# Pinning the adaLN dot-product passes behind the weights' subtractions on VectorE

## The chip, the cores and the metric

One core of a Trainium2 chip runs the whole kernel in one launch. The metric is device time in microseconds; lower is better. All inputs are in HBM in fp32 and the output is written back there.

## The reference, cut to what matters

Two layers work on 256 latent and 256 context tokens of width 2048. Each layer modulates its normalised input with vectors that are a matrix product of a conditioning vector and a large weight (adaLN), goes through a wide projection, a mixer and an output projection:

```python
for layer in range(DEPTH):                       # 2
    shift, scale, gate = split(silu(c) @ ada_w[layer] + ada_b[layer], 3)      # ada_w: 2048 x 6144
    h = rms_norm(x, pre_g[layer]) * (1.0 + scale) + shift                     # the same for ctx with c_ctx
    if layer % 2 == 0:
        y = pool_conv_mixer(h, ev_w_in, ..., ev_w_out)   # 2048 -> 6144, mixer, 2048 -> 2048
    else:
        y, yc = hgrn2_mixer(h, hc, od_w_in, ..., od_w_out)
    x = x + gate * rms_norm(y, post_g[layer])
```

`silu(c) @ ada_w` has only two rows (latent and context), so it is a matrix-vector product for each of two vectors; every weight is used twice.

## The kernel before, in words

Activations stand as 16 tiles of 128 features by 512 tokens. Every large product is done in three TensorE matmuls of 128x512 for each 128x128 block (`mm3`, lines 172 to 174): the fp32 weight tile `raw` is split into a rounded part `whi` (a cast on ScalarE, line 131) and a rest `wlo` (**the weights' subtraction** on VectorE, line 132), and the products whi·x_hi, whi·x_lo and wlo·x_hi are added in PSUM. The third matmul, L174, is the only one that needs `wlo`.

- **Weights' stream.** `order` lists every weight load of the program; `weights()` hands out the next split tile and `ahead()` starts the load, the cast and the subtraction of the one after it. `raw`, `whi` and `wlo` have 3 buffers each. `proj_tile` computes one output tile of 128 features in two **halves**; a half takes one weight tile of 128x1024 and 24 matmuls.
- **Stages.** First the group product of 7 feature tiles (`main0`, weights `evg`), then feature tiles 7 to 47 of the even layer's input projection (weights `ev`, 82 halves), with the pooling mixer (`finish_a`, lines 500 to 561) and the convolution mixer (`finish_b`, lines 571 to 582) in between; then its output projection (weights `evo`, 16 tiles, 32 halves; `yin` is its input, lines 627 to 635 gather sums of each tile); then the odd layer.
- **adaLN on VectorE.** Part of the adaLN products is no TensorE work: `ada_dve` (line 257) loads transposed weights `adat` 128x1024 at a time into the two buffers `raw2` (512 KB each; `loads` asks for the next one before it hands out the last) and multiplies and sums each with `srow`, once for each of the two vectors: `tensor_tensor_reduce`, line 270, called **a pass** here. The profile shows a pass as a custom instruction that writes `ajunk` and a short accumulator read behind it. One load with its two passes is called **a part**. There are 104 parts, 208 passes. `step(n)` runs the next n parts at places in the source: six in the last `main0` calls, two in each half from feature tile 7 on until the first 16 are done, then, with `hook0`, one in the second half of feature tiles 12, 13 and 17, one in each half from feature tile 18 on, and one in each half of the output projection until they are used up. `add_shift` (lines 420 and 421) adds a shift to h around the end of feature tile 11 and needs the first 16 parts.
- **Order.** A scheduler at build time puts each engine's instructions in a fixed order by its own estimate of when their inputs are there. Nothing ties a pass to its place in the source: it may stand before or after subtractions and mixer work of other places. On the chip each engine and the queue of loads on SyncE run strictly in the order built.

Of the kernel before, what the change touches and what calls it, by code (L numbers as in the profile page):

```python
# [12 lines left out]
ALU = mybir.AluOpType  # L13
# [34 lines left out]
def block_kernel(ctx: ExitStack, tc: tile.TileContext, par, xt, invcnt, poolw, ada, adat, crow, evg, evb, ev, evo,  # L48
                 odg, odz, odi, odo, rows, out):
    nc = tc.nc  # L50
    V, S, GP, T = nc.vector, nc.scalar, nc.gpsimd, nc.tensor
# [9 lines left out]
    def mm_ps(nm="mmps"):  # L61
        return ps.tile([P, 512], F32, name=nm, tag="mm", bufs=5)

    def aux_ps(shape, nm):
        return ps.tile(shape, F32, name=nm, tag="aux", bufs=3)
# [49 lines left out]
    def loads(srcs):  # L115

        t = None
        for src in srcs:
            nx = load(src, "raw2", 2)
            if t is not None:  # L120
                yield t
            t = nx
        yield t
# [91 lines left out]
    def ada_end(l, t, k0, tr):  # L215

        nk, nv = tr.shape[1:]
        ks = slice(k0, k0 + nk)
        m = mod[:, l, t, ks, 0:nv]
        V.tensor_tensor(m, tr, ada_b[:, l, t, ks].unsqueeze(2).broadcast_to([P, nk, nv]), op=ALU.add)  # L220
        if t == 0:
            return
        if t == 1:
            V.tensor_scalar(m, m, 1.0, None, op0=ALU.add)
        g = (pre_g if t == 1 else post_g)[:, l, ks]
        V.tensor_tensor(m, m, g.unsqueeze(2).broadcast_to([P, nk, nv]), op=ALU.mult)
# [26 lines left out]
    srow = a0.tile([P, 2, D], F32, name="srow")  # L253
# [6 lines left out]
    def ada_dve(units):  # L260

        parts = [(l, t, 4 * u + i, half) for l, t, u in units for i in range(4) for half in range(2)]
        srcs = [adat[ADAT[l, t], n, :, half * 1024:half * 1024 + 1024] for l, t, n, half in parts]
        for (l, t, n, half), raw in zip(parts, loads(srcs)):
            i = n % 4
            if not i and not half:
                sums = a0.tile([P, 2, 4, 2], F32, name="asum", bufs=2)
            for v in range(2):
                junk = a0.tile([P, 1024], BF16, name="ajunk")
                V.tensor_tensor_reduce(junk, raw, srow[:, v, half * 1024:half * 1024 + 1024], 1.0,  # L270
                                       sums[:, 0, i, v:v + 1] if half else 0.0, op0=ALU.mult, op1=ALU.add,
                                       accum_out=sums[:, half, i, v:v + 1])
            if half and i == 3:
                ada_end(l, t, n - 3, sums[:, 1])
            yield
# [69 lines left out]
    def ada_raw(l, t, u, s):  # L345
        raw = big_tile([P, 4, 1024], F32, "adaraw")
        for g in range(0, 4, 2):
            nc.sync.dma_start(raw[:, g:g + 2, :],
                              ada[l, t, u, 4 * s + g:4 * s + g + 2].rearrange("g p n -> p g n"))
        return raw  # L350
# [25 lines left out]
    for u in range(1, 4):  # L376
        acc = aux_ps([P, P], "adaps")
        for s in range(2):
# [5 lines left out]
            raw = ada_raw(0, 1, u, s)  # L384
# [5 lines left out]
        make_h0(range(4 * u, 4 * u + 4))  # L390

    job = ada_dve([(0, 0, u) for u in range(2, 4)])

    for u in range(2):
        acc = aux_ps([P, P], "adaps")
        for s in range(2):
            raw = ada_raw(0, 0, u, s)
# [62 lines left out]
    def bias_job():  # L460
# [7 lines left out]
        yield  # L468

    job = ada_dve([(0, 2, u) for u in range(4)] + [(1, t, u) for u in range(4) for t in (1, 0) if t == 0 or u < 3])  # L470

    LP = 8
# [181 lines left out]
    sums = [mm_ps("stps") for _ in range(3)]  # L654
# [414 lines left out]
    half = [[mm_ps() for _ in range(2)] for _ in range(2)]  # L1069
# [16 lines left out]
    half = [[mm_ps(), aux_ps([P, 512], "mmx")], [aux_ps([P, 512], "mmx") for _ in range(2)]]  # L1086
# [112 lines left out]
```

## Time and profile before

| | us |
|---|---|
| median of 3 runs | 1710.59 (1707.89 to 1714.49) |
| profiled execution, device time | 1711.67 |
| its span, first to last instruction | 1710.0 |
| TensorE busy | 1648.6 (96%) |
| TensorE weight loads busy | 1356.4 (79%) |
| VectorE busy | 1193.2 (70%) |
| ScalarE busy | 595.8 (35%) |
| bytes moved | 295.28 MB, mean 173 GB/s |

The profiled execution lies 1.1 us above the median and 1.67 us of it are outside the span. Busy time is the union of instructions on an engine; matmul records overlap (a 128x512 matmul is shown as 0.39 us though the next starts 0.23 us later), so a busy TensorE is not one at its peak. "Idle before" is put down to what ended it.

### The profile page before, as it was taken

The page shows a single profiled execution, that of the slowest core. Times are in us where ns is not written, and L with a number is a line of the kernel's source. Part 1 is how long each engine was busy: PE and PEld are TensorE (multiplying, and loading weights), DVE is VectorE, ACT ScalarE, POOL GpSimd, SP SyncE. Part 2 cuts the span into 40 slices and gives each one's busy share as a digit, 9 for nine tenths or more (in the row PEclk, how much of TensorE's full clock was granted, in tenths as well). Part 3 has the DMA queues.
Part 4 walks back from the last instruction along what each step waited for, and adds up shares of the span by engine and source line. Part 5 has one row for each costly group of instructions (what it writes and reads, how often), then busy time and mean ns, then how long its engine had stood idle before and what let it go on. Part 6 is the DMA issues. An engine that isn't in the chain of part 4 may idle for free.

```text
span 1710.0 us, 23085 instructions
## 1 busy us (share of the span) xinstructions
PE 1648.6 (96%) x8878; PEld 1356.4 (79%) x8878; DVE 1193.2 (70%) x2079; ACT 595.8 (35%) x944; POOL 79.3 (5%) x154
## 2 busy tenths in 40 slices
PE   7999999998999999999799999999999999999997
PEld 4777778876777788887688888888888888888886
DVE  3459988998888844444996873778648774566755
ACT  4323533322122223332353432343323332434543
POOL 0000000000000000001300000000000100000000
PEclk9999999999999999999899999999999999999999
DMA  9986466666666663333266542545425333333453
GB/s 355 351 333 223 153 217 196 209 220 211 221 208 213 214 255 108 99 99 121 67 169 180 166 156 86 179 148 183 143 87 186 116 103 107 114 120 112 167 183 130
DMA packets 98046, 295.28 MB, mean 173 GB/s; under 512 B 26000, under 2 KB 26128, under 8 KB 96272
## 3 DMA queue, kind: packets, MB, share of 16 engines
q1 hardware_dynamic: 97936, 293.82, 52.0%
q8 instruction: 69, 1.13, 0.3%
q14 instruction: 41, 0.34, 0.1%
HBM read 289.58 MB, written 4.19 MB: 172 GB/s over the span
## 4 chain that ended last, share of the span: by engine, by line
PE 66%; DVE 15%; DMA 13%; issue 5%; POOL 0%; ACT 0%; SPq 0%; DVEq 0%; POOLq 0%; ACTq 0%
PE mmps L172 12%; PE mmps L173 12%; PE mmps L174 12%; DMA raw<-adat_dram 9%; PE mmps L191 5%; DVE ajunk L270 5%; PE mmps L952 3%; PE mmps L954 3%; PE mmps L953 3%; DVE wlo L132 3%; PE mmps L192 3%; DMA raw<-ada_dram 1%; DMA adaraw<-ada_dram 1%; PE adaps L212 1%; PE mmps L1061 1%
## 5 line engine op out<-in xcount | busy, mean ns | idle before, releaser
L132 DVE TENSOR_TENSOR wlo<-raw,whi 128x1024 fp32r<-128x1024 f32 (+3 forms) x328 | 388.6, 1187 | 284.7 <-ACT whi L131 277.6
L131 ACT CAST whi<-raw 128x1024 fp32r<-128x1024 f32 (+3 forms) x328 | 334.3, 1024 | 720.6 <-PE mmps L173 455.7
L174 PE MATMUL mmps<-h,wlo 128*128 128x512 f32 x1216 | 478.2, 394 | 22.7 <-DVE wlo L132 22.6
L172 PE MATMUL mmps<-h,whi 128*128 128x512 f32 x1216 | 479.4, 395 | 7.2 <-ACT h L710 6.6
L173 PE MATMUL mmps<-h,whi 128*128 128x512 f32 x1216 | 478.6, 394 | 3.8 <-DVE h L711 3.6
L174 PEld LDWEIGHTS mmps<-h,wlo 128*128 128x128 f32 x1216 | 230.1, 189 | 80.0 <-DVE wlo L132 32.3
L172 PEld LDWEIGHTS mmps<-h,whi 128*128 128x128 f32 x1216 | 230.2, 189 | 58.3 <-ACT h L710 7.2
L173 PEld LDWEIGHTS mmps<-h,whi 128*128 128x128 f32 x1216 | 230.5, 190 | 52.6 <-DVE h L711 4.9
L191 PE MATMUL mmps<-h,whi 128*128 128x512 f32 x496 | 177.9, 401 | 0.0
L270 DVE CUSTOM_DVE_ANT_0 ajunk<-raw,srow,asum 128x1024 bf16<-128x1024 f32 x104 | 133.4, 1283 | 30.4 <-DMA raw<-adat_dram 29.1
L192 PE MATMUL mmps<-h,wlo 128*128 128x256 f32 x496 | 139.4, 281 | 1.3 <-DVE wlo L132 1.3
L270 DVE CUSTOM_DVE_ANT_0 ajunk<-raw,srow 128x1024 bf16<-128x1024 f32 x104 | 127.1, 1222 | 16.9 <-DMA raw<-adat_dram 16.0
L191 PEld LDWEIGHTS mmps<-h,whi 128*128 128x128 f32 x496 | 93.1, 188 | 23.0 <-issue 0.5
L952 PE MATMUL mmps<-whi,h 128*128 128x512 f32 x256 | 100.1, 391 | 0.0
L954 PE MATMUL mmps<-wlo,h 128*128 128x512 f32 x256 | 99.8, 390 | 0.0
L953 PE MATMUL mmps<-whi,h 128*128 128x512 f32 x256 | 99.8, 390 | 0.0
L172 PE MATMUL mmps<-yin,whi 128*128 128x512 f32 x256 | 99.6, 389 | 0.0
L173 PE MATMUL mmps<-yin,whi 128*128 128x512 f32 x256 | 99.6, 389 | 0.0
L174 PE MATMUL mmps<-yin,wlo 128*128 128x512 f32 x256 | 99.6, 389 | 0.0
L192 PEld LDWEIGHTS mmps<-h,wlo 128*128 128x128 f32 x496 | 93.6, 189 | 2.6 <-DVE wlo L132 2.0
L954 PEld LDWEIGHTS mmps<-wlo,h 128*128 128x128 f32 x256 | 48.1, 188 | 10.2
L174 PEld LDWEIGHTS mmps<-yin,wlo 128*128 128x128 f32 x256 | 48.1, 188 | 10.0
(271 smaller groups left out, 1966.9 us busy)
## 6 DMA issues: line engine op xcount, KB each, us to landing
raw<-odz_dram SPq DMA_DIRECT2D x118, 512.0 KB, 3.3
raw<-adat_dram SPq DMA_DIRECT2D x104, 512.0 KB, 4.6
raw<-ev_dram SPq DMA_DIRECT2D x82, 512.0 KB, 4.5
adaraw<-ada_dram SPq DMA_DIRECT2D x24, 1024.0 KB, 8.9
raw<-ada_dram SPq DMA_DIRECT2D x36, 512.0 KB, 4.3
raw<-evo_dram SPq DMA_DIRECT2D x32, 512.0 KB, 3.4
raw<-odi_dram SPq DMA_DIRECT2D x32, 512.0 KB, 3.4
raw<-odo_dram SPq DMA_DIRECT2D x32, 512.0 KB, 3.3
```

What stands on the lines that cost most here:

```text
L131: S.copy(hi[:, 0:n], raw[:, 0:n])
L132: V.tensor_tensor(lo[:, 0:n], raw[:, 0:n], hi[:, 0:n].bitcast(F32), op=ALU.subtract)
L172: T.matmul(o, whi, xhi, start=first, stop=False)
L173: T.matmul(o, whi, xlo, start=False, stop=False)
L174: T.matmul(o, wlo, xhi, start=False, stop=last)
L191: T.matmul(o, whi, xhl, start=first, stop=False)
L192: T.matmul(o[:, 0:SEQ], wlo, xhl[:, 0, :], start=False, stop=last)
L212: T.matmul(acc[32 * j:32 * j + 32, :], vec[:, k, :], rv[:, i, j, :], start=k == 0, stop=k == KT - 1, tile_position=(0, 32 * j))
L270: V.tensor_tensor_reduce(junk, raw, srow[:, v, half * 1024:half * 1024 + 1024], 1.0, sums[:, 0, i, v:v + 1] if half else 0.0, op0=ALU.mult ...
L952: T.matmul(o, xh[:, c], hi[:, w], start=k == 0, stop=False)
L953: T.matmul(o, xl[:, c], hi[:, w], start=False, stop=False)
L954: T.matmul(o, xh[:, c], lo[:, w], start=False, stop=k == KT - 1)
```

## The change

Each pass is wrapped in a call that adds an edge of order, without a wait, from the instruction traced just before it on VectorE. A pass can then not be placed ahead of anything that the source has before it on VectorE; what the source has behind it can still be placed ahead of it.

```diff
             for v in range(2):
                 junk = a0.tile([P, 1024], BF16, name="ajunk")
-                V.tensor_tensor_reduce(junk, raw, srow[:, v, half * 1024:half * 1024 + 1024], 1.0,
-                                       sums[:, 0, i, v:v + 1] if half else 0.0, op0=ALU.mult, op1=ALU.add,
-                                       accum_out=sums[:, half, i, v:v + 1])
+                tc.keep_in_program_order(V.tensor_tensor_reduce(
+                    junk, raw, srow[:, v, half * 1024:half * 1024 + 1024], 1.0, sums[:, 0, i, v:v + 1] if half else 0.0,
+                    op0=ALU.mult, op1=ALU.add, accum_out=sums[:, half, i, v:v + 1]))
```

The instructions are the same ones; their order moves. VectorE in the middle of the even layer's input projection, before (L132 is a weights' subtraction, a row that writes ajunk is a pass, the row behind it its accumulator read, other lines are mixer work):

```order
L132 TENSOR_TENSOR wlo<-raw,whi 128x1024
L270 ISA ajunk,asum<-raw_3411,srow 128x1024
L270 ISA asum 128x1
L270 ISA ajunk,asum<-raw_3411,srow 128x1024
L270 ISA asum 128x1
L270 ISA ajunk,asum<-raw_3447,srow,asum 128x1024
L270 ISA asum 128x1
L270 ISA ajunk,asum<-raw_3447,srow,asum 128x1024
L270 ISA asum 128x1
L132 TENSOR_TENSOR wlo<-raw,whi 128x1024
```

The same passes with the change:

```order
L132 TENSOR_TENSOR wlo<-raw,whi 128x1024
L270 ISA ajunk,asum<-raw_3411,srow 128x1024
L270 ISA asum 128x1
L270 ISA ajunk,asum<-raw_3411,srow 128x1024
L270 ISA asum 128x1
L132 TENSOR_TENSOR wlo<-raw,whi 128x1024
L270 ISA ajunk,asum<-raw_3447,srow,asum 128x1024
L270 ISA asum 128x1
L270 ISA ajunk,asum<-raw_3447,srow,asum 128x1024
L270 ISA asum 128x1
L571 TENSOR_TENSOR ubuf_1756<-mmps,bc 128x256 x2
L132 TENSOR_TENSOR wlo<-raw,whi 128x1024
```

Where two to four passes stood between two subtractions, two stand now, all the way down the stage. Between the subtraction of feature tile 20's second half and that of tile 47's second half there were 154 passes, and there are 110. VectorE in the output projection, before (L630 and L635 are the sums of a finished tile):

```order
L132 TENSOR_TENSOR wlo<-raw,whi 128x1024 x2
L630 TENSOR_TENSOR sqy<-yb,xb 128x512
L635 TENSOR_TENSOR acc_4896<-acc_4896,sqy 128x512
L635 TENSOR_TENSOR acc_4897<-acc_4897,sqy 128x512
L635 TENSOR_TENSOR acc_4898<-acc_4898,sqy 128x512
L132 TENSOR_TENSOR wlo<-raw,whi 128x1024 x2
```

With the change:

```order
L132 TENSOR_TENSOR wlo<-raw,whi 128x1024
L630 TENSOR_TENSOR sqy<-yb,xb 128x512
L635 TENSOR_TENSOR acc_4896<-acc_4896,sqy 128x512
L635 TENSOR_TENSOR acc_4897<-acc_4897,sqy 128x512
L635 TENSOR_TENSOR acc_4898<-acc_4898,sqy 128x512
L270 ISA ajunk,asum<-raw_5154,srow,asum 128x1024
L270 ISA asum 128x1
L270 ISA ajunk,asum<-raw_5154,srow,asum 128x1024
L270 ISA asum 128x1
L132 TENSOR_TENSOR wlo<-raw,whi 128x1024
L270 ISA ajunk,asum<-raw_5190,srow 128x1024
L270 ISA asum 128x1
```

Before, no pass stood here; now 54 do, two behind each subtraction of output tiles 0 to 13. On SyncE's queue the `adat` loads move along: 154 and 110 passes mean 77 and 55 loads beside the `ev` loads, and 27 now alternate with the `evo` loads, on both sides of the four 1 MB loads of `xb` (line 614). VectorE around `add_shift` (L421), before:

```order
L435 COPY sh_pad<-mod 128x16x2
L523 COPY pm<-pm 128x256
L270 ISA ajunk,asum<-raw_1796,srow 128x1024
L270 ISA asum 128x1
L132 TENSOR_TENSOR wlo<-raw,whi 128x1024
L421 SCALAR_TENSOR_TENSOR h_195<-xr,mod,h_193 128x256 x16
L421 SCALAR_TENSOR_TENSOR h_196<-xr,mod,h_194 128x256 x9
L270 ISA ajunk,asum<-raw_1798,srow,asum 128x1024
L270 ISA asum 128x1
L421 SCALAR_TENSOR_TENSOR h_196<-xr,mod,h_194 128x256 x7
L132 TENSOR_TENSOR wlo<-raw,whi 128x1024 x3
```

With the change:

```order
L132 TENSOR_TENSOR wlo<-raw,whi 128x1024
L220 TENSOR_TENSOR mod<-asum,pt 128x8
L421 SCALAR_TENSOR_TENSOR h_195<-xr,mod,h_193 128x256 x16
L421 SCALAR_TENSOR_TENSOR h_196<-xr,mod,h_194 128x256 x9
L435 COPY sh_pad<-mod 128x16x2
L501 COPY psum_w<-psum_w 128x2
L500 TENSOR_TENSOR psum_w<-psum_w 128x556
L421 SCALAR_TENSOR_TENSOR h_196<-xr,mod,h_194 128x256 x7
L501 COPY psum_w<-psum_w 128x4
L521 TENSOR_TENSOR pm<-psum_w 128x128
L132 TENSOR_TENSOR wlo<-raw,whi 128x1024 x2
```

The passes of later parts (raw_1796, raw_1798) left this place, and some pooling work took theirs.

## Rows read from the trace of the kernel before

**Rows 1.** The page: busy time, and shares of the chain that ended last.

```profile
PE 1648.6 (96%) x8878; PEld 1356.4 (79%) x8878; DVE 1193.2 (70%) x2079; ACT 595.8 (35%) x944; POOL 79.3 (5%) x154
...
PE mmps L172 12%; PE mmps L173 12%; PE mmps L174 12%; DMA raw<-adat_dram 9%; PE mmps L191 5%; DVE ajunk L270 5%; PE mmps L952 3%; PE mmps L954 3%; PE mmps L953 3%; DVE wlo L132 3%; PE mmps L192 3%; DMA raw<-ada_dram 1%; DMA adaraw<-ada_dram 1%; PE adaps L212 1%; PE mmps L1061 1%
```

**Rows 2.** Busy time by stretch: columns as in the first row.

```profile
core 0: us, PE busy (x) PEld busy (x) DVE busy (x) ACT busy (x) POOL busy (x), PEclk, DMA share, GB/s
...
245.00:370.00 125.00, 125.00 (x552) 103.30 (x551) 114.13 (x191) 38.35 (x55) 0.00 (x0) 1.00 0.64 204
370.00:592.00 222.00, 203.99 (x863) 162.35 (x863) 193.26 (x301) 46.92 (x54) 0.00 (x0) 0.98 0.67 214
592.00:800.00 208.00, 207.69 (x917) 171.71 (x916) 95.38 (x125) 69.44 (x104) 0.00 (x0) 1.00 0.39 132
```

**Rows 3.** Costliest groups in 370 to 592 us.

```profile
L174 PE MATMUL mmps<-h,wlo 128*128 128x512 f32 x287 | 115.1, 401 | 18.0 <-DVE wlo L132 17.9
...
L270 DVE CUSTOM_DVE_ANT_0 ajunk<-raw,srow,asum 128x1024 bf16<-128x1024 f32 x55 | 70.6, 1284 | 19.2 <-DMA raw<-adat_dram 18.4
L270 DVE CUSTOM_DVE_ANT_0 ajunk<-raw,srow 128x1024 bf16<-128x1024 f32 x54 | 66.0, 1222 | 9.5 <-DMA raw<-adat_dram 8.9
...
L132 DVE TENSOR_TENSOR wlo<-raw,whi 128x1024 fp32r<-128x1024 f32 x36 | 43.9, 1220 | 0.0
```

**Rows 4.** Waits of VectorE in 370 to 592 us: total, times, longest.

```profile
DVE ajunk L270 <- DMA raw<-adat_dram: 27.3, 33, 1.8
```

**Rows 5.** Timeline, 382 to 392 us: start, duration, engine, instruction, idle before it.

```profile
382.44 1.05 ACT L131 CAST whi<-raw 128x1024 fp32r<-128x1024 f32 x1 [4.34 <-PE mmps L173]
...
384.69 1.22 DVE L270 CUSTOM_DVE_ANT_0 ajunk<-raw,srow 128x1024 bf16<-128x1024 f32 x1
...
387.21 1.28 DVE L270 CUSTOM_DVE_ANT_0 ajunk<-raw,srow,asum 128x1024 bf16<-128x1024 f32 x1 [1.29 <-DMA raw<-adat_dram]
...
389.75 1.22 DVE L132 TENSOR_TENSOR wlo<-raw,whi 128x1024 fp32r<-128x1024 f32 x1
...
391.02 0.50 PE L174 MATMUL mmps<-h,wlo 128*128 128x512 f32 x1 [2.48 <-DVE wlo L132]
```

**Rows 6.** TensorE by windows: us, PE busy (x), clock, DMA share, GB/s.

```profile
440.00:450.00 10.00, 9.66 (x36) 0.83 0.71 224
450.00:460.00 10.00, 10.00 (x46) 1.00 0.73 237
```

**Rows 7.** Weights and adat loads in 370 to 592 us: time from issue to landing.

```profile
DMA to landing us min/median/max: 3.2/4.6/6.5
```

**Rows 8.** VectorE in 660 to 704 us, costliest groups: four output tiles.

```profile
L132 DVE TENSOR_TENSOR wlo<-raw,whi 128x1024 fp32r<-128x1024 f32 x9 | 11.0, 1225 | 28.3 <-ACT whi L131 28.3
L635 DVE TENSOR_TENSOR acc<-acc,sqy 128x512 f32<-128x512 f32 x12 | 7.6, 684 | 0.0
L630 DVE TENSOR_TENSOR sqy<-yb,xb 128x512 f32<-128x512 f32 x4 | 2.7, 684 | 0.0
```

**Rows 9.** Busy time by stretch in the output projection, columns as in rows 2.

```profile
620.00:640.00 20.00, 20.00 (x90) 16.58 (x89) 7.36 (x9) 7.08 (x10) 0.00 (x0) 1.00 0.84 326
640.00:700.00 60.00, 60.00 (x267) 49.69 (x266) 26.62 (x35) 20.31 (x31) 0.00 (x0) 1.00 0.33 106
```

**Rows 10.** Timeline of TensorE and VectorE before and around add_shift.

```profile
130.70 0.50 PE L174 MATMUL mmps<-h,wlo 128*128 128x512 f32 x1 [1.08 <-DVE wlo L132]
...
179.61 9.99 DVE L421 SCALAR_TENSOR_TENSOR h<-xr,mod,h 128x256 fp32r<-128x256 f32 x25
...
193.49 3.50 DVE L132 TENSOR_TENSOR wlo<-raw,whi 128x1024 fp32r<-128x1024 f32 x3
...
194.77 0.53 PE L174 MATMUL mmps<-h,wlo 128*128 128x512 f32 x1 [3.35 <-DVE wlo L132]
```

**Rows 11.** Waits of VectorE in 120 to 245 us: total, times, longest.

```profile
DVE wlo L132 <- ACT whi L131: 4.2, 3, 2.4
```

## The prediction

> **What bounds the kernel now.** I read the page first. TensorE is busy for 1648.6 of 1710.0 us, so idle time alone offers 61 us; but the chain that ended last spends 9% of the span on `adat` loads, 5% on passes and 3% on subtractions [rows 1]. That names a place where TensorE waits for VectorE, which waits for a load of the adaLN job.
>
> Busy time by stretch shows where [rows 2]. From 592 to 800 us TensorE does 917 matmuls in 208 us, from 245 to 370 us 552 in 125 us: 0.2268 and 0.2264 us each, the rate of a fed engine. From 370 to 592 us it does 863 in 222 us. At 0.2266 us they need 195.6 us, so **26.4 us are lost in this stretch**. The 863 are 36 halves of 24 matmuls: 6.17 us for a half where 5.44 would do.
>
> The costliest groups of that stretch say who is late [rows 3]. The only TensorE group that waits is L174, the matmul that needs `wlo`: 18.0 us, all but 0.1 put down to the subtraction. VectorE does 36 subtractions and 55 + 54 = 109 passes there, three for each half where the source has two. It is busy for 193.26 us [rows 2] and waits 27.3 us for `adat` loads [rows 4]: 220.6 of 222 us. So VectorE, with those waits, is the bound here and TensorE follows.
>
> One stall in the timeline [rows 5] shows how. The cast of a weight tile ends at 383.49 us, so its subtraction could start. Two passes stand ahead of it, then 1.29 us of waiting for the next part's load, then two more passes; the subtraction starts at 389.75 us, and TensorE stands idle 2.48 us until 391.02.
>
> The matmul-busy row shows 18.0 us of idle, the count of matmuls 26.4. The rest lies in matmul records that overlap across a stall and in the clock: granted 0.98 in the stretch [rows 2], a loss of at most 222 x 0.02 = 4.4 us; in 440 to 450 us, behind one stall of 2 us, it is 0.83 and 36 matmuls pass in 9.66 busy us, 46 in the 10 us after at 1.00 [rows 6]. If only the visible idle came back, the gain would be 18 us and the time 1693. I take the count. The Trainium skill, in Perfetto Trace Analysis, Identifying the Most-Contended Engine, says that matmul busy time is a bad measure and that weight-load busy time should be read. By that rule, 162.35 us of weight loads against 171.71 in 208 us of a fed stretch [rows 2] would need 196.7 us, a loss of 25.3; the trace agrees with the rule and not with the busy row.
>
> **The change, part by part.**
>
> *Projection of the even layer, 370 to 592 us.* No instruction is added or removed. Between subtractions stand two passes instead of three on average, so these 36 halves lose 109 - 72 = 37 passes. A pass lasts 1.22 or 1.28 us [rows 3]; at 1.25, 46 us leave, and VectorE has 193.3 - 46 = 147 us of work, 4.1 us in each half of 5.44. The subtraction comes first in its half, and 1.3 us are over. The waits for loads shrink as well. A part now takes 222 / 54.5 = 4.07 us, so a `raw2` buffer comes round every 8.15 us, of which its two passes take 2.5 and a load 4.6 [rows 7], with about 1 us of waiting and issue between. At a part for each half it comes round every 10.88 us, 2.7 us later than now, against a mean wait of 27.3 / 54.5 = 0.5 us [rows 4] and a longest of 1.8. I expect all 26.4 us back.
>
> *Moved into the output projection: 27 parts.* They land on 592 to 800 us, where VectorE is busy for 95 of 208 us [rows 2]. An output tile takes TensorE 10.88 us. VectorE there has two subtractions, 2.45 us, and sums of (7.6 + 2.7) / 4 = 2.6 us [rows 8]; four passes of 1.25 make it 10.0. That is tight but fits, and the cover is deeper than the 0.9 us: with three buffers a cast may begin when the third half back is through, 10.9 us before its tile is needed, so after cast and subtraction (1.05 and 1.22 us, [rows 5]) some 8.6 us of lead remain. Cost taken: nothing. If that cover fails and each part waits the 0.83 us of a wait now (27.3 / 33, [rows 4]), a tile takes 11.66 us and 13.5 tiles lose 10.5 us; this is the lower end.
>
> *Loads.* On SyncE's queue the 27 `adat` loads alternate with `evo` loads and stand before and behind the 4 MB of `xb`. Per half that is 0.52 MB more in 5.44 us, 96 GB/s on top of 106 [rows 9]; the stretch before moves 214 [rows 2]. While `xb` comes, 326 GB/s are moved with TensorE full [rows 9]; one `adat` load ahead of the next weights there costs 0.52 MB / 326 GB/s = 1.6 us of the 8.6 us lead. Cost: nothing. What waits behind a late pass is the next subtraction, then L174.
>
> *Before and around add_shift, 128 to 195 us.* Two stalls stand here: 1.08 us at 130.70 and 3.35 us at 194.77, where the subtraction at 193.49 came behind the whole of `add_shift`, 179.61 to 193.5 [rows 10]. With the change two passes fewer stand ahead of `add_shift` and one fewer inside it, but pooling work of about the length of a pass moves in, and passes can no longer fill VectorE's time before a late subtraction; it waits 4.2 us for casts here now [rows 11]. So this place lies between +4.4 us (both stalls gone) and -4.2 us (those waits once more, on the path). I take +1: the early stall goes, since the pooling work ahead of that subtraction now stands behind it, and the later one stays.
>
> **Sum.** 26.4 + 1 = 27.4 us off the profiled execution's 1711.67: 1684.3. The median of the runs lies 1.1 lower, so the forecast is **1683 us**. Its ends: 26.4 + 4.4, about 1680, or 1678 with a clock that no longer drops behind the late stall; and 26.4 - 4.2 - 10.5, 1699.
>
> **Rivals.**
>
> *The buffers bind, not the order (no change).* VectorE's waits are for a load into one of two `raw2` buffers, and ScalarE's cast in [rows 5] had waited 4.34 us for TensorE to free a `whi` buffer. If buffer turns pace the stage, reordered passes meet the same waits in other places, and the time stays near 1711 (1702 to 1719). For it: 27.3 us of waiting for loads [rows 4]. Against: TensorE ran full from 245 to 370 us with the same buffers [rows 2], and the turn needed, 8.15 us, is under 10.88. The Trainium skill, in Perfetto Trace Analysis, Optimization Strategy, reads a gap that repeats on the engine that should be full as a sign that there may be too little SBUF for the next tile. By that rule this rival would be the likeliest; the trace bears it out only for the stall's size, not its place. Here too belongs the case that the new order does move but that another wait of equal size appears.
>
> *A pinned pass holds what it waits for (slower).* SyncE's queue is in order. An `adat` load now stands behind a weight load that waits for a `raw` buffer, which a subtraction frees; and a pass that waits for that load stands ahead of the next subtraction. If loads come late this way, each part waits w. In the projection a half then takes 4.1 + w, which costs beyond w = 1.3; an output tile takes 10.0 + 2w, which costs beyond w = 0.45. At w = 1.4 the output projection loses 13.5 x (12.8 - 10.88) = 26 us and 55 halves of the projection 3: the gain is gone; that is the point. At 1.8, the longest wait now [rows 4], 13.5 x 2.72 + 55 x 0.46 = 62 us are lost, 35 more than gained: 1745 us. Against it: the mean wait is 0.5 at a faster turn, and a load has 2.7 us more time.
>
> **How the numbers follow.** Forecast 0.77, from 1678 to 1699; no change 0.12; slower by the pinned wait 0.07; a gain of some 9 to 12 us, between forecast and no change, 0.04. A measurement here can tell 0.5%, 8.6 us, from nothing, so faster is 0.77 + 0.04 = 0.81, same 0.12, slower 0.07. The range goes from 1677 to 1702, which holds the forecast and most of the 0.04.
>
> **What would show it.** In the profile after, TensorE's rate from 245 us to the end of the projection should be 0.2266 us per matmul with the clock at 1.00 and nearly no wait of L174 for `wlo`; `adat` off the chain; VectorE near 75% in the projection and 90% in the output projection, where passes now run until about its twelfth tile. I am wrong if L174 waits for `wlo` in the output projection, if passes still wait a microsecond each for `adat`, or if the stall around `add_shift` grows past 5 us.

## The result, and the profile after

The changed kernel takes **1687.18 us** (median of 4 runs, 1686.03 to 1688.43) against 1710.69 for the kernel before in the same comparison: a ratio of 0.9861, 95% interval 0.9841 to 0.9882, so 23.5 us faster. Forecast were 1683 us, between 1677 and 1702. The profiled execution of the change took 1686.03 us, with a span of 1684.3, 25.7 us less than before.

The page of the changed kernel, busy time and shares of the chain, against [rows 1]:

```profile
PE 1641.8 (97%) x8878; PEld 1355.5 (80%) x8878; DVE 1195.4 (71%) x2079; ACT 597.5 (35%) x944; POOL 79.4 (5%) x154
...
PE mmps L173 19%; PE mmps L174 19%; PE mmps L172 19%; PE mmps L191 6%; PE mmps L952 3%; PE mmps L954 3%; PE mmps L953 3%; PE mmps L192 3%; DMA adaraw<-ada_dram 1%; PE adaps L212 1%; PE mmps L1060 1%; PE mmps L1061 1%; PE mmps L1059 1%; DVE wlo L132 1%; PE mmx L173 1%
```

Every engine does what it did. The `adat` loads and the passes, 9% and 5% of the chain before, are gone from it, and the main matmuls rise from 12% to 19% a line.

Busy time by stretch of the changed kernel, columns as in [rows 2]:

```profile
245.00:370.00 125.00, 125.00 (x578) 102.99 (x578) 100.72 (x165) 40.54 (x56) 0.00 (x0) 1.00 0.58 184
370.00:592.00 222.00, 222.00 (x981) 183.81 (x980) 169.92 (x256) 55.09 (x61) 0.00 (x0) 1.00 0.62 194
...
640.00:700.00 60.00, 60.00 (x266) 49.67 (x266) 53.15 (x81) 20.47 (x32) 0.00 (x0) 1.00 0.60 192
```

From 370 to 592 us TensorE passes 981 matmuls instead of 863, 222 / 981 = 0.2263 us each, at a clock of 1.00 (the 2.4 GHz level). VectorE is at 77% there. In the output projection, where it was at 44% [rows 9], it is at 53.15 of 60 us, 89%, and TensorE is as full as before.

Costliest groups and VectorE's waits from 370 to 592 us, against [rows 3, 4]:

```profile
L174 PE MATMUL mmps<-h,wlo 128*128 128x512 f32 x327 | 127.2, 389 | 0.0
...
L270 DVE CUSTOM_DVE_ANT_0 ajunk<-raw,srow,asum 128x1024 bf16<-128x1024 f32 x42 | 53.8, 1282 | 0.8
L132 DVE TENSOR_TENSOR wlo<-raw,whi 128x1024 fp32r<-128x1024 f32 x41 | 50.2, 1225 | 46.7 <-ACT whi L131 46.2
L270 DVE CUSTOM_DVE_ANT_0 ajunk<-raw,srow 128x1024 bf16<-128x1024 f32 x40 | 48.8, 1220 | 0.3
```

41 subtractions stand against 82 passes, two for each half. L174 waits 0.0 us instead of 18.0, the passes no longer wait for `adat`, and it is now the subtraction that waits, 46.2 us for the casts: VectorE runs ahead of TensorE.

A timeline of the changed kernel, ScalarE's cast and VectorE, against [rows 5]:

```profile
378.23 1.05 ACT L131 CAST whi<-raw 128x1024 fp32r<-128x1024 f32 x1 [4.34 <-PE mmps L173]
379.31 1.22 DVE L132 TENSOR_TENSOR wlo<-raw,whi 128x1024 fp32r<-128x1024 f32 x1 [1.76 <-ACT whi L131]
380.46 1.28 DVE L270 CUSTOM_DVE_ANT_0 ajunk<-raw,srow,asum 128x1024 bf16<-128x1024 f32 x1
381.78 1.28 DVE L270 CUSTOM_DVE_ANT_0 ajunk<-raw,srow,asum 128x1024 bf16<-128x1024 f32 x1
383.67 1.06 ACT L131 CAST whi<-raw 128x1024 fp32r<-128x1024 f32 x1 [4.38 <-PE mmps L173]
```

The subtraction follows its cast at once, 1.08 us behind its start. Before, the subtraction at 389.75 that TensorE waits for [rows 5] came 12.7 us behind the start of its own cast. That cast is not the one at 382.44 in [rows 5], which belongs to the next tile, but the one ahead of it: casts and subtractions are 328 each, with the same widths in the same order. The kernel before:

```profile
377.05 1.05 ACT L131 CAST whi<-raw 128x1024 fp32r<-128x1024 f32 x1 [4.41 <-DMA raw<-ev_dram]
```

**A marker for all runs.** ScalarE casts the weight tiles in one order in every kernel. Where a cast waited for TensorE to free its buffer (`<-PE mmps L173` below), its start tells how far TensorE is; the 60th and the 100th cast, counted from 0, wait so in every run here. Two casts that lie 40 halves apart in the projection (the 60th and the 100th), before:

```profile
359.40 1.06 ACT L131 CAST whi<-raw 128x1024 fp32r<-128x1024 f32 x1 [4.34 <-PE mmps L173]
...
604.50 1.06 ACT L131 CAST whi<-raw 128x1024 fp32r<-128x1024 f32 x1 [4.34 <-PE mmps L173]
```

and with the change:

```profile
361.91 1.05 ACT L131 CAST whi<-raw 128x1024 fp32r<-128x1024 f32 x1 [4.34 <-PE mmps L173]
...
579.51 1.05 ACT L131 CAST whi<-raw 128x1024 fp32r<-128x1024 f32 x1 [4.34 <-PE mmps L173]
```

Before, the 40 halves took 245.1 us, 6.13 each; now 217.6, 5.44 each. So 27.5 us were gained in these **40 halves**, after 2.5 us had been lost ahead of the first of them. Of the 25.0 nothing is given back in the output projection, whose matmuls take 173.8 us from the first to the last in both kernels (626.3 to 800.1 us and 601.3 to 775.1 us), and 0.7 come later.

### The profile page after: what moved, and what is told of

The parts are those of the page before. It is cut to its first block, busy times and chain, and to the rows that moved or that the text cites. A ratio compares the mean times of both kernels' runs of the same rounds, so it can differ in the third digit from the quotient of the medians.

```text
span 1684.3 us, 23062 instructions
## 1 busy us (share of the span) xinstructions
PE 1641.8 (97%) x8878; PEld 1355.5 (80%) x8878; DVE 1195.4 (71%) x2079; ACT 597.5 (35%) x944; POOL 79.4 (5%) x154
## 4 chain that ended last, share of the span: by engine, by line
PE 91%; DVE 5%; DMA 3%; issue 1%; ACT 0%; POOL 0%; SPq 0%; DVEq 0%; POOLq 0%; ACTq 0%
PE mmps L173 19%; PE mmps L174 19%; PE mmps L172 19%; PE mmps L191 6%; PE mmps L952 3%; PE mmps L954 3%; PE mmps L953 3%; PE mmps L192 3%; DMA adaraw<-ada_dram 1%; PE adaps L212 1%; PE mmps L1060 1%; PE mmps L1061 1%; PE mmps L1059 1%; DVE wlo L132 1%; PE mmx L173 1%
## 5 line engine op out<-in xcount | busy, mean ns | idle before, releaser
L132 DVE TENSOR_TENSOR wlo<-raw,whi 128x1024 fp32r<-128x1024 f32 (+3 forms) x328 | 388.8, 1187 | 291.3 <-ACT whi L131 283.8
L173 PE MATMUL mmps<-h,whi 128*128 128x512 f32 x1216 | 477.0, 392 | 3.8 <-DVE h L711 3.7
L174 PE MATMUL mmps<-h,wlo 128*128 128x512 f32 x1216 | 475.2, 391 | 3.5 <-DVE wlo L132 3.5
L174 PEld LDWEIGHTS mmps<-h,wlo 128*128 128x128 f32 x1216 | 229.2, 188 | 53.3 <-DVE wlo L132 4.4
L173 PEld LDWEIGHTS mmps<-h,whi 128*128 128x128 f32 x1216 | 229.8, 189 | 52.1 <-DVE h L711 5.0
L173 PE MATMUL mmps<-yin,whi 128*128 128x512 f32 x256 | 99.6, 389 | 0.0
L174 PE MATMUL mmps<-yin,wlo 128*128 128x512 f32 x256 | 99.6, 389 | 0.0
L174 PEld LDWEIGHTS mmps<-yin,wlo 128*128 128x128 f32 x256 | 48.0, 188 | 10.1
```

The lines of the kernel that those rows point to most:

```text
L132: V.tensor_tensor(lo[:, 0:n], raw[:, 0:n], hi[:, 0:n].bitcast(F32), op=ALU.subtract)
L173: T.matmul(o, whi, xlo, start=False, stop=False)
L174: T.matmul(o, wlo, xhi, start=False, stop=last)
```

## The experiments

Three jobs, each on one chip with the kernel before beside it (medians of before: 1708.74, 1704.77 and 1703.90 us). The ratios are those on record, with their intervals; the quotient of the medians differs from them by up to 0.0014.

| run | median us | ratio to before, 95% | the 40 halves, us |
|---|---|---|---|
| pins on the first 16 parts | 1710.56 | 1.0014 (1.0003 to 1.0026) | 244.4 |
| pins on the other 88 | 1681.48 | 0.9854 (0.9838 to 0.9870) | 217.6 |
| the change, one part free | 1683.23 | 0.9860 (0.9846 to 0.9874) | 217.6 |
| the change, thin passes | 1689.88 | 0.9898 (0.9881 to 0.9914) | 217.6 |
| before, with room (control) | 1704.21 | 0.9993 (0.9981 to 1.0005) | 238.6 |
| before, room, 3 buffers, no pin | 1676.20 | 0.9830 (0.9805 to 0.9856) | 217.6 |
| change, room, 3 buffers | 1676.38 | 0.9830 (0.9806 to 0.9854) | 217.6 |
| change, 3 parts per output tile | 1703.53 | 0.9989 (0.9975 to 1.0002) | 217.6 |
| change, 3 passes per half | 1710.32 | 1.0034 (1.0021 to 1.0047) | 237.2 |
| the same, room, 3 buffers | 1675.76 | 0.9833 (0.9816 to 0.9850) | 217.6 |
| pins on the 88, room, 3 buffers | 1675.70 | 0.9832 (0.9818 to 0.9846) | 217.6 |
| the change again | 1688.85 | 0.9907 (0.9893 to 0.9920) | 217.6 |

The first four are one job, the next four the second, the last four the third.

### Where the gain is made: the first parts or the others

```diff
-                tc.keep_in_program_order(V.tensor_tensor_reduce(...))
+                ins = V.tensor_tensor_reduce(...)
+                if len(units) == 2:
+                    tc.keep_in_program_order(ins)
```

The first 16 parts are a job of two units; the second run has `> 2` in its place.

> Only the 16 parts that add_shift needs are pinned; the other 88 float as before. Order theory (the passes that stand three and four at a time ahead of a subtraction make the loss of 370 to 592 us): three passes stand for each half there as before, so the time stays near the kernel before, 1706 to 1714 us, with some 26 us still lost in that stretch. Rival (the gain comes from the start, a schedule that begins in another way and stays ahead): most of the 23 us gain comes with this pin, below 1695 us.

> Only the other 88 parts are pinned; the first 16 float as before. Order theory: all 26 us of 370 to 592 us come back, and the early stall before add_shift is as before (1.1 us at 130 us instead of 1.8): 1684 to 1688 us, at most 1.5 us faster than the change. Rival (the gain comes from the start): less than half of it, above 1699 us.

Pins on the first 16 parts alone give nothing: the 40 halves take 244.4 us. Pins on the other 88 give all of it, 217.6. The rival of a better start falls. The second run went below its range, 1681.48, and its profile is 5.7 us shorter than the change's, 3.8 of it by the 60th cast; but the two come from different jobs, and by the ratios (0.9854 against 0.9861) they can't be told apart. What differs in the profiles is `add_shift`; pins on the 88, VectorE and TensorE there:

```profile
177.41 12.76 DVE L423 SCALAR_TENSOR_TENSOR h<-xr,mod,h 128x256 fp32r<-128x256 f32 x32
...
190.09 2.35 DVE L132 TENSOR_TENSOR wlo<-raw,whi 128x1024 fp32r<-128x1024 f32 x2
...
191.36 0.50 PE L174 MATMUL mmps<-h,wlo 128*128 128x512 f32 x1 [0.34 <-DVE wlo L132]
```

`add_shift` (L423 here, two lines further down) starts 2.2 us earlier than before [rows 10], nothing stands inside it, and the stall behind it shrinks to 0.34 us. (Its bias stage, next section, gains nothing: it waits 7.8 us for loads, the change's 5.2.) With the change:

```profile
179.56 9.99 DVE L421 SCALAR_TENSOR_TENSOR h<-xr,mod,h 128x256 fp32r<-128x256 f32 x25
...
190.41 2.86 DVE L421 SCALAR_TENSOR_TENSOR h<-xr,mod,h 128x256 fp32r<-128x256 f32 x7
...
194.73 0.60 PE L174 MATMUL mmps<-h,wlo 128*128 128x512 f32 x1 [2.97 <-DVE wlo L132]
```

### The part that holds a buffer through the bias stage

Behind `add_shift` the kernel loads biases through the same two `raw2` buffers.

```diff
-                tc.keep_in_program_order(V.tensor_tensor_reduce(...))
+                ins = V.tensor_tensor_reduce(...)
+                if (l, t, n, half) != (0, 2, 1, 0):
+                    tc.keep_in_program_order(ins)
```

> The change, but the part that stands behind the bias stage (latent gate, feature tile 1, first half) is not pinned. Theory of the missing 1.4 us: this part's pinned passes hold one of the two raw2 buffers through the bias stage, so that the bias loads go through one buffer; freed, TensorE's waits for bias loads fall from 5.2 us to about 2.4 and the time by 1 to 2.5 us, to 1685 to 1686. Rival (the 1.4 us are the casts and subtractions at 130 us, or add_shift): no change, within 0.7 us of the change.

TensorE's instructions at L212, 200 to 260 us: first and last start and what they waited for, the change:

```profile
L212 PE MATMUL biasps<-raw,sh_pad x128: 272/273/297, 214.7 to 251.2; 128*32 128x128 f32 x128
...
  DMA raw<-evb_dram: 5.2, 6
```

and with the part freed:

```profile
L212 PE MATMUL biasps<-raw,sh_pad x128: 272/273/298, 215.4 to 236.8; 128*32 128x128 f32 x128
...
  DMA raw<-evb_dram: 1.4, 3
```

The bias stage ends 14 us earlier and waits 1.4 us instead of 5.2 (before: 2.4). From the 26th cast to the 60th this run needs 186.1 us, the change 187.6, before 185.5: 1.6 us of the change's loss ahead of 360 us. That the pinned part lengthens these waits is shown; what it costs in time is not, since the ratio, 0.9860, cannot be told from the change's in the first comparison.

### Do the passes cost anything now?

```diff
-                    junk, raw, srow[:, v, half * 1024:half * 1024 + 1024], ...
+                    junk[:, 0:64], raw[:, 0:64], srow[:, v, half * 1024:half * 1024 + 64], ...
```

> The change, with each pass cut to 64 of its 1024 columns; the loads are whole. The output is wrong in the adaLN vectors by what is left out. It takes some 240 us of work from VectorE. If the passes lie beside other work everywhere now, as the forecast took it (cost nothing in the projection and in the output projection), the time falls by 0 to 5 us, all of it ahead of 200 us. If the moved passes cost something in the output projection where VectorE is at 88%, or still do in the projection, it falls by 8 us or more, there.

From 370 us to the end of the output projection the thin passes change nothing, with VectorE at 40% instead of 77%:

```profile
370.00:592.00 222.00, 222.00 (x981) 183.80 (x981) 89.85 (x256) 55.08 (x61) 0.00 (x0) 1.00 0.56 194
```

From the 60th cast to the 140th both kernels need 454.2 us, so the moved passes cost nothing there, as the sum had it. (Cutting them took 202 us of busy time from VectorE, 1195.4 to 993.8, not 240.) But the whole is not 0 to 5 us faster, and neither theory had that: the profile is 4.3 us longer than the change's, and 4.0 of it are lost by the 60th cast, though the times can't tell the two apart (0.9898 lies between 0.9861 and 0.9907, the change's two ratios). The weights come late. Waits of ScalarE's casts from 125 to 190 us, thin passes:

```profile
ACT whi L131 <- DMA raw<-ev_dram: 26.8, 6, 8.1
```

The change has no such wait, and its loads from 100 to 165 us take 4.9 us to land in the median, these 6.1. ScalarE's half of `add_shift` (L420) then starts at 183.54 us instead of 175.70, the next casts stand behind it, and TensorE pays in one stall:

```profile
197.91 0.79 PE L172 MATMUL mmps<-h,whi 128*128 128x512 f32 x1 [5.89 <-ACT whi L131]
```

Why the weights come late stays open. VectorE frees the `raw2` buffers sooner here, so `adat` loads may take bandwidth from the weights' loads. But the built order differs too: from 131 to 158 us two `adat` loads stand ahead of each `ev` load on SyncE's queue, where with the change it is mostly one. No run parts the two.

### Buffers or order

Room for a third `raw2` buffer was made by sharing other buffers; the control has the room alone, without the last two lines. The main edits, shortened:

```diff
-        vbuf = [l0.tile([P, BW], F32, name="vbuf0")]
-        ubuf = [l0.tile([P, 515], F32, name="ubuf0")]
+        vbuf = [l0.tile([P, BW], F32, name="vbuf0", tag="edge")]
...
+        ubuf = [l0.tile([P, BW], F32, name="ubuf0", tag="edge")]
...
-        r = bd.tile([P, 1024], F32, name="araw", bufs=2)
+        r = bd.tile([P, 1024], F32, name="araw", bufs=1)
...
-        ... load(src, "raw2", 2) ... load(ada[1, t, 3, g], "raw2", 2)
+        ... load(src, "raw2", 3) ... load(ada[1, t, 3, g], "raw2", 3)
```

> The kernel before with 4 KB for each partition freed by sharing buffers elsewhere (the edges of the two mixers share one, the odd layer's adaLN loads go through one extra buffer instead of two), which the next kernel needs. Control: within 4 us of the kernel before.

> The control with three raw2 buffers instead of two; nothing is pinned and three passes still stand for each half. Buffers theory: the 27 us of waiting for adat loads and with them the whole 26 us loss go; as fast as the change, 1688 us or less. Order theory, with the waits as one half of it: the passes alone fill 193 of the 195.6 us that the stretch needs, so the waits shrink and the subtractions still come behind three or four passes; some of the loss goes, 1692 to 1704 us. If loads behind late weights on the queue make the waits, and not the number of buffers: no change, over 1706.

> The change with the room edits and three raw2 buffers. Order theory: in the projection nothing is left to gain; at most the bias stage gains its 1 to 2.5 us: 1684 to 1688 us. Buffers theory: buffers still hold the changed kernel back, and it gains 5 us or more.

The control stayed where it was expected (1704.21 against 1704.77). The next run upset my reading. **Without any pin, a third buffer takes the whole loss away.** Before with room and three buffers, 370 to 592 us:

```profile
370.00:592.00 222.00, 222.00 (x981) 183.85 (x980) 196.45 (x306) 54.52 (x61) 0.00 (x0) 1.00 0.68 226
```

and its costliest groups there:

```profile
L174 PE MATMUL mmps<-h,wlo 128*128 128x512 f32 x327 | 127.2, 389 | 0.0
L270 DVE CUSTOM_DVE_ANT_0 ajunk<-raw,srow,asum 128x1024 bf16<-128x1024 f32 x53 | 68.0, 1283 | 1.1
L270 DVE CUSTOM_DVE_ANT_0 ajunk<-raw,srow 128x1024 bf16<-128x1024 f32 x52 | 63.5, 1222 | 0.8
...
L132 DVE TENSOR_TENSOR wlo<-raw,whi 128x1024 fp32r<-128x1024 f32 x41 | 50.1, 1221 | 19.3 <-ACT whi L131 19.2
```

VectorE does as much as in the kernel before (196.45 us against 193.26 [rows 2]), two to four passes still stand between most subtractions until the last pass, and TensorE is full: L174 waits 0.0 us. What has gone is the waiting for `adat`: none is listed here, against 30.0 us in the control from 245 to 592 us. With three buffers the pin adds nothing (0.9830 both). So passes that stand ahead of subtractions do not cost by themselves. The buffers theory was right for this run, and the order theory's 1692 to 1704 wrong. For the run with pins the order theory gave 1684 to 1688; its 1676.38, more than 5 us below the change, is what the buffers theory said, but the gain is not in the projection: the 40 halves take 217.6 us as with the change, and 7.5 us are gained ahead of them. That is the start of `add_shift`, 176.84 us instead of 179.56, and the bias stage, which waits 1.3 us for loads instead of 5.2.

### The same rate with pins

If the loss is the rate of passes against the turn of two buffers, it must come back with pins and a higher rate, and go with a third buffer. Both runs keep every pass pinned:

```diff
             elif half or n >= 18:
-                step(1)
+                step(1 + (half and n >= 18))
```

> The change, every pass pinned, but the source now asks for two parts instead of one in the second half of feature tiles 18 to 47: three passes for each half, the rate that the kernel before had by itself; two raw2 buffers. Rate theory (the loss is this rate against the turn of two buffers, 8.15 us for two parts where 7.25 are to be had; the pin helped only because it lowers the rate): the loss comes back though no pass passes a subtraction of the source, some 25 us over the 40 halves from the 60th to the 100th cast (6.1 us a half instead of 5.44), 1704 to 1714 us in all. Order theory (passes that run ahead of their place make the loss): it stays gone, 1683 to 1690 us.

> The same with three raw2 buffers and the room edits. Rate theory: three buffers turn in 12.2 us at this rate, more than the 8.15 that a part takes: no loss between the 60th and the 100th cast (217.6 us), 1675 to 1684 us. Order theory: as with two buffers, within 4 us of the run before.

Three passes per half, two buffers, 370 to 592 us, busy time:

```profile
370.00:592.00 222.00, 208.56 (x895) 169.84 (x894) 199.15 (x314) 49.19 (x57) 0.00 (x0) 0.97 0.67 221
```

and its waits there:

```profile
DVE ajunk L270 <- DMA raw<-adat_dram: 22.0, 32, 1.4
PE mmps L174 <- DVE wlo L132: 13.4, 5, 5.9
```

No pass stands ahead of its place in the source, though one to six stand between two subtractions, since a later subtraction may still be placed ahead of a pass. The loss is back under the pin: 19.6 us in the 40 halves (237.2 - 217.6; expected some 25) and 1710.32 us in all. That the whole falls into its range is in part luck: against the change on the same chip another 3.9 us are lost from the 100th cast to the 140th, where the last passes run on to 616 us, 1.1 ahead of the 60th and 1.2 behind the 140th. With three buffers it is gone:

```profile
370.00:592.00 222.00, 222.00 (x981) 183.82 (x980) 208.12 (x328) 54.87 (x61) 0.00 (x0) 1.00 0.73 241
```

VectorE is busy for 208 of 222 us here, and TensorE still waits for nothing. Gaps of up to five passes stand here too. The rate theory gave both times, the order theory neither. (A part is wanted every 3.63 us here, so three buffers come round in 10.9 us, not in 12.2 as expected; that is still more than 8.15.)

### What the cover in the output projection is worth

```diff
-            elif half or n >= 18:
+            elif half or n >= 18 and n % 2:
...
-        proj_tile(t, act_y, lambda half: step(n + half > 0))
+        proj_tile(t, act_y, lambda half: step(2 if half else n > 0))
```

> The change with the places of the parts moved: one half in four of feature tiles 18 to 47 gets none, and a tile of the output projection gets three parts instead of two, so six passes. By the forecast's sum VectorE then needs 6 x 1.25 + 2.45 + 2.6 = 12.55 us for an output tile that takes TensorE 10.88: 14 tiles lose 23 us, less a lead of 8.6 us that is used up once: 15 to 23 us slower than the change, 1702 to 1710 us, with L174 waiting for wlo there. If parts also wait for their loads as in the kernel before, 0.8 us each, 14 x 2.5 us more: 1735 to 1745. If the passes cost nothing there at all: as the change, 1687.

Busy time with three parts per output tile:

```profile
640.00:700.00 60.00, 58.67 (x260) 48.25 (x259) 57.83 (x92) 20.30 (x31) 0.00 (x0) 1.00 0.61 203
700.00:800.00 100.00, 89.41 (x475) 71.49 (x473) 83.54 (x136) 28.74 (x47) 0.00 (x0) 0.93 0.57 190
```

and the waits from 640 to 800 us:

```profile
PE mmps L174 <- DVE wlo L132: 11.5, 4, 4.8
DVE ajunk L270 <- DMA raw<-adat_dram: 7.4, 12, 1.0
```

The input projection is as fast as with the change; from the 100th cast to the 140th it needs 254.8 us instead of 236.6, 18.2 more, inside 15 to 23. Against the change, from another job, it is 0.0128 x 1704.77 = 22 us slower by the ratios, 14 by the change's other ratio, 0.9907, and 16 by the medians. So the total of the sum, 12.55 us per tile less the lead, was about right; but the loss came in four waits of L174 and a clock that fell to 0.93, nearly all behind 700 us, not a little with each tile, and passes did wait for loads, 7.4 us, which the sum left out.

### A version that beats both

> Three raw2 buffers with the room edits, and pins only on the 88 parts behind add_shift. If what three buffers gain beyond the change (0.983 against 0.986) and what the unpinned first parts gain at add_shift are separate, 1 to 3 us faster than three buffers with all pins: a ratio of 0.981 to the kernel before. If both are the same stall at add_shift: 0.983.

> The change itself, on the chip of the three others, so that they can be set against it: 0.986 of the kernel before.

Three buffers with pins on the 88 take 1675.70 us (runs 1675.43 to 1675.97), the change on the same chip 1688.85 (1686.11 to 1689.46): 13.2 us less. The three-buffer kernels cannot be told apart (0.9830 to 0.9833), so the free first parts add nothing to the third buffer. That fits both having removed the same stall at `add_shift`: from 186 to 198 us TensorE waits for nothing in this kernel or in the change with three buffers, where the change waits 2.97 us. The simplest of the versions is the kernel before with the third buffer and no pin.

The change again gave 0.9907, not 0.986. Its own time hardly differs from the first comparison (1688.85 against 1687.18); the kernel before took 1703.90 us here and 1710.69 there. So the gain was 15 us in one job and 24 in the other. The profile of the control fits that: its passes wait 30.0 us for `adat` from 245 to 592 us where the kernel before waited 37.6, and its 40 halves lose 21.0 us, not 27.5. What differs between the jobs, each on another chip, was not tried, and that it is their loads stays open.

## Why the prediction was right, and where its reason was not

**All 26.4 us back: right.** 222 us passed 981 matmuls, 0.2263 us each, against 0.2266 forecast. The marker gives 27.5 us for 40 halves, 23 us more of the program than the stretch. The count of matmuls was the right measure: the visible idle, 18.0 us, would have given 1693. The weight-load measure of the Trainium skill (Perfetto Trace Analysis, Identifying the Most-Contended Engine) gave 25.3 us; it and the count lie too close for these runs to part them. But of the step's two halves only one was needed. That 46 us of passes leave VectorE is not what freed TensorE: with three buffers and no pin VectorE stays at 196.45 us of 222, and nothing is lost. That a buffer comes round later, so that the waits go, is.

**One reading was off.** The cast at 382.44 us is not that of the subtraction at 389.75; its own cast ended at 378.10, so it came 11.7 us late and not 6.3. The passes and the wait ahead of it are as told.

**Moved into the output projection at no cost: right.** VectorE is at 89% there (forecast 90%), the last pass ends at 739 us, in the thirteenth output tile (about the twelfth), and the thin passes gained nothing. The run with three parts per tile shows how near the edge was.

**Loads at no cost: right** in both projections: passes wait 0.5 us for `adat` from 245 to 592 us and not at all from 592 to 760. Not counted were the bias loads: the pinned part behind the bias stage holds a buffer, and its waits rose from 2.4 to 5.2 us.

**Before and around add_shift, +1: wrong in sign.** By the 60th cast 2.5 us were lost. The step said that the early stall goes, since the pooling work ahead of that subtraction stands behind it. It did not go. TensorE, 128 to 132 us, the change, against [rows 10]:

```profile
129.78 0.50 PE L172 MATMUL mmps<-h,whi 128*128 128x512 f32 x1 [1.24 <-ACT whi L131]
...
131.04 0.50 PE L174 MATMUL mmps<-h,wlo 128*128 128x512 f32 x1 [0.53 <-DVE wlo L132]
```

That is 1.24 + 0.53 = 1.77 us, where 0.33 + 1.08 = 1.41 stood before. The cast itself is late: ScalarE starts it at 128.69 us instead of 127.80, behind two copies on its own queue, one of them for the pooling (L494, 127.90 us). So the step looked at the pooling work on VectorE alone. The later stall went from 3.35 to 2.97, and the rest is about the bias stage's 2.8 us more of waiting. -2.5 lies between the ends given, +4.4 and -4.2.

**The sum.** 27.5 - 2.5 + 0.7 = 25.7 us off the span, 27.4 forecast. The profiled execution came to 1686.03 instead of 1684.3; the other 2.5 us of the miss are that it lies 1.15 us below its median, where that of before lay 1.1 above.

**The rivals.** "The buffers bind, not the order (no change)" had the right cause and the wrong result, and my argument against it failed: that TensorE ran full from 245 to 370 us with the same buffers, and that a turn of 8.15 us is under 10.88. A turn of 10.88 us is to be had only once the rate has fallen to a part for each half, which is what the pin does; at three passes for each half two parts are wanted every 7.25 us. And from 245 to 370 us TensorE ran full because VectorE was still using up its lead. Casts of that stretch at 266.97 (below) and 359.40 us (shown above), and their subtractions:

```profile
266.97 1.06 ACT L131 CAST whi<-raw 128x1024 fp32r<-128x1024 f32 x1 [3.05 <-PE mmps L173]
...
269.80 1.22 DVE L132 TENSOR_TENSOR wlo<-raw,whi 128x1024 fp32r<-128x1024 f32 x1
...
369.81 1.22 DVE L132 TENSOR_TENSOR wlo<-raw,whi 128x1024 fp32r<-128x1024 f32 x1
```

The subtraction starts 2.8 us behind its cast at first and 10.4 us behind it at the end; at 12.7 us TensorE stands. So the buffers did bind, and the pin helped by asking less of them. To choose between order and buffers was wrong: the unpinned order set the rate, the two buffers made the rate cost something, and either cure is enough (217.6 us in every run with at most one part per half, or with three buffers). The rule of the Trainium skill (Perfetto Trace Analysis, Optimization Strategy), that a gap which repeats can mean too little SBUF for the next tile, pointed to the cause; the third buffer, 0.9830 without a pin, agrees with it. I was wrong to weigh it only against the place of the stall. "A pinned pass holds what it waits for" did not come: passes wait 0.5 us in all from 245 us on, where w = 1.4 for each part was its point.

## What to carry to other kernels

When filler work waits for loads on the engine that feeds the bound engine, compare the time in which its buffers come round with the time in which it asks for them: a lower rate or one more buffer does the same, and the buffer needs no order. An edge of order that helps does not show that the order was the cause; bring the old rate back under the new order and cure the old order in another way, as two runs did here. And a pin on work whose load has filled a buffer pins the buffer too, so look at who else uses it until that place.

## What was not expected of the hardware

- VectorE as a feeder can be 94% busy (208.12 of 222 us) without TensorE losing anything, and at 87% (193.26 of 222) TensorE lost 26 us: the 27.3 us of waits for loads decided, not the share of busy time.
- Passes cut to a sixteenth did not make the kernel faster (0.9898 against 0.9861 and 0.9907 of the change); its profile loses 4.0 us by the 60th cast, with loads that took 6.1 us to land instead of 4.9. Why is open.
- The kernel before differs by 0.4% between the jobs, each on one chip (1703.90 to 1710.69 us), the changed one by 0.1% (1687.18 and 1688.85).
